# A hybrid decoder trunk on one core: the norm vector moved from the weights to x, keys joined in pairs, and a list schedule with other priorities

## The chip, the core and the metric

The kernel runs on one core of one Trainium2 chip, as one launch. The metric is the device time of a launch in microseconds (us), the median over several runs.

## The reference

The computation is a trunk of two residual layers over 1,024 positions of width 1,024, in float32. The first (even) layer splits one input projection into sliding-window attention and a state-space mixer (S5); the second (odd) layer is stick-breaking attention. Each is followed by a SwiGLU feed-forward network (FFN) of width 2,816.

```python
hn = rmsnorm(x, even_norm[i])          # x * rsqrt(mean(x^2) + eps) * gain
proj = hn @ even_w_in[i]
q, k, v, u = jnp.split(
    proj, [SWA_WIDTH, SWA_WIDTH + KV_WIDTH, SWA_WIDTH + 2 * KV_WIDTH], axis=-1)
q = rmsnorm(q.reshape(b, l, SWA_Q_HEADS, HEAD_DIM), q_norm[i])
k = rmsnorm(k.reshape(b, l, SWA_KV_HEADS, HEAD_DIM), k_norm[i])
o_attn = swa_sink_attention(q, k, v, sinks[i])
o_ssm = s5_mixer(u, ...)
mixed = jnp.concatenate([o_attn, o_ssm], axis=-1) @ even_w_out[i]
...
x = x + mixed
hn = rmsnorm(x, ffn_norm[layer])
x = x + (jax.nn.silu(hn @ ffn_w_gate[layer]) * (hn @ ffn_w_up[layer])) @ ffn_w_down[layer]
```

## The kernel before, in words

Every large product is made of three TensorE products of rounded operands: each operand is split into a high part (`hi`) and the rest (`lo`), and `mm3` (L301 to L305) adds high x high, high x low and low x high. The high part is a copy on ScalarE (ACT) or VectorE (DVE), the low part a subtraction on DVE or, for some weights, on GpSimd (POOL). TensorE (PE) also does the transposes, by a product with the identity.

**Who sets the order.** The kernel is written as tasks with an engine, an assumed duration, dependencies, tokens for buffers, and a priority `pos`. `Flow.run` (L133) is a list scheduler: it plays the tasks through once, and each time an engine is free by its assumed durations it takes the ready task with the lowest `pos` whose tokens are there. What it takes is emitted at once, so that the order of every engine, and of the DMA issues on SyncE (SP), is fixed when the kernel is built. The assumed durations only set the order; on the chip each engine goes through its list and waits where a dependency isn't met. The priorities hang on a table of constants (L59 to L77: `WKVPOS`, `S5POS`, `SWAPOS`, `LEAD`, `EVAC`, `POS1` and others).

**The even layer**, in which the edits lie (`even`, L735):

1. *Norm and transposes* (`norm`, L769). Each of the 8 tiles of x (128 rows, 512 KB) is loaded (`xt`, two buffers, L774), squared and summed on ACT (L779), and its reciprocal root `r` is made by `rstd_tasks` (L361): one small step on DVE (L367), Ln and Exp on ACT, three or four small steps on DVE (L378 to L383), and a copy into `rx` (L782). The tile itself is transposed unscaled (`psT`, L788) and split into `hh` and `hl` (L269 or L267, L795). The factor r is applied later, to the results.
2. *Weights* (`weight_tasks`, L308). The norm vector (gain) is folded into the weights of this layer. For keys and values ACT and DVE do it in four pieces each (L328, L344); for u and q POOL scales the loaded block in four pieces (`scaled`, L338), ACT takes the high part (L331) and POOL the low part (L348).
3. *Keys and values* (`kv`, L856), one tile at a time, each in a PSUM bank: 24 products (`ps_kv`), evacuation on ACT (L872, L873), a sum (L877), the root by `rstd_tasks`, the scaling of the keys on DVE (L880), one transpose (`ps_kT`, L886), a copy.
4. *u* (`u_round`, L929, twice), *q* (`q_round`, L1012, twice), each with two blocks of weights.
5. *S5* (`s5_common`, L389, then eight `s5_eighth`, L596). `s5_common` is one chain on DVE, from the transposed angles (`ps_a`, L436; the first DVE row is L441) to the tables (L541); the first product that needs it is the transpose `ps_v` (L622).
6. *Sliding-window attention* (`swa`, L1155, eight tiles: scores `ps_s`, exponentials on ACT, `ps_pT`, `ps_o`), and the *GLU* of S5 (`ps_g`, L1285; sigmoid on ACT). Exp and Sigmoid lie in different ACT table sets; `Trunk.act` (L243) puts a table load (L249) wherever the set changes in ACT's order.
7. *Output projection* in two halves (`ps_wo`), then the norm of half 0 with its transposes (`psT`, L1515, `hn`), then that of half 1 with the sums for the FFN (`T`, L1596 to L1613).

The FFNs (`ps_gu`, L1679, and `ps_d`, L2013) and the odd layer (`odd_tasks`, L2086) follow in the same schedule. The two FFNs are dense stretches of 128x512 products.

Of the kernel before, what the change touches and what calls it, by code (L numbers as in the profile page):

```python
# [107 lines left out]
class Flow:  # L108
# [110 lines left out]
class Trunk:  # L219
# [88 lines left out]
    def weight_tasks(self, fl, src, a, b, pos, deps=(), engines=("POOL", "POOL"), wtok=("w8",),  # L308
                     rtok=("raw",), gain=None, pool=None, tile_=None):
# [13 lines left out]
        def hi():  # L323
            st["w"] = tile_() if tile_ else (pool or self.wp).tile([P, 2, a, b], F32R, tag="w8", name="w8")
            if folded:
                for k in range(4):
                    part = slice(m * k, m * k + m)
                    nc.scalar.activation(out=st["w"][:, 0, part], in_=st["raw"][:, part], func=AF.Copy,  # L328
                                         scale=gain[:, k:k + 1])
            elif engines[0] == "ACT":  # L330
# [4 lines left out]
        def scaled():
            for k in range(4):
                part = st["raw"][:, m * k:m * k + m]
                nc.gpsimd.tensor_scalar(out=part, in0=part, scalar1=gain[:, k:k + 1], scalar2=None, op0=ALU.mult)  # L338

        def lo():  # L340
            if folded:
                for k in range(4):
# [1 line left out]
                    nc.vector.scalar_tensor_tensor(out=st["w"][:, 1, part], in0=st["raw"][:, part],  # L344
                                                   scalar=gain[:, k:k + 1], in1=st["w"][:, 0, part].bitcast(F32),
                                                   op0=ALU.mult, op1=ALU.subtract)
                return
# [387 lines left out]
    def even(self, right):  # L735
# [22 lines left out]
        fl.tokens(xt=XT, uc=1, uT=2, t1=1, el=1, cl=2, kp=1, tp=2, rot=1, sv=1, gv=1, gw=1,  # L758
                  hv=1, yg=1, pT=2, sq=1, qn=1, kv=2)
# [8 lines left out]

        def norm(t, pos):  # L769
# [6 lines left out]
            def square():  # L776
                sq = npool.tile([P, DM], F32, tag="xn", name="xn", bufs=1)
                st["ss"] = self.smp.tile([P, 1], F32, tag="ss", name="ss")
                A.activation(out=sq, in_=st["xt"], func=AF.Square, accum_out=st["ss"])  # L779

            def keep():
                V.tensor_copy(out=rx[:, t:t + 1], in_=st["r"])  # L782

            def turn(kh):
                st[kh] = bank("B", [P, 4, P], "psT")
                for j in range(4):
# [1 line left out]
                    nc.tensor.transpose(st[kh][:, j], st["xt"][:, k * P:(k + 1) * P], self.ident)  # L788
# [1799 lines left out]
```

## Time and profile before

| what | value |
|---|---|
| median of 3 runs | 2378.26 us (2377.5 to 2378.88) |
| profiled execution, its own time | 2380.52 us |
| its span, first to last instruction | 2378.7 us |
| PE busy in the span | 2295.7 us |
| DVE, ACT, POOL busy | 1594.0, 1036.4, 598.4 us |
| granted TensorE clock, mean | 0.985 |

The profile is of one execution. A row of the timeline gives start, duration, engine, line, operation, and in brackets the idle time of the engine before it with what released it. A row of the stages gives for each engine the busy time in that stretch and the number of instructions; PEclk is the share of full clock that TensorE was granted. 1.8 us of the profiled time lie outside the span. PE is the busiest engine, and its idle time, 83.0 us in all, is what another order can save.

### The profile page before, as it was taken

To read this page: it belongs to the slowest core of one execution; us is meant where nothing else is said; L and a number is where in the kernel's file an instruction comes from. 1 tells how busy PE (TensorE), PEld (TensorE's weight loads), DVE (VectorE), ACT (ScalarE), POOL (GpSimd) and SP (SyncE) were. 2 spreads that over 40 slices of the span, in tenths; PEclk is the share of its full clock that TensorE was granted. 3 is DMA by queue.
4 is the path that set the end of the run, shared out by engine and by line. 5 is a ranking of instruction groups with operands and counts; after the bars stand their busy time and mean duration, and the time that the engine had idled before them with its cause. 6 is when DMAs were issued, how large, how long until landed. Compare 5 with 4: busy or idle time off the path is not lost.

```text
span 2378.7 us, 32679 instructions
## 1 busy us (share of the span) xinstructions
PE 2295.7 (97%) x12284; PEld 1854.1 (78%) x12284; DVE 1594.0 (67%) x2514; ACT 1036.4 (44%) x2070; POOL 598.4 (25%) x526
## 2 busy tenths in 40 slices
PE   7897999999999999999999999999989999999998
PEld 6796488888888887777877777788768888888777
DVE  7998655755555558884676766778655655556785
ACT  6276843422222233354565655665423222233332
POOL 4310000553434324400000000000243534333530
PEclk9998999999999999999999999999989999999999
DMA  5110225332323284334211111235422323248333
GB/s 148 32 36 23 75 89 196 106 106 91 114 93 115 93 309 169 98 103 128 76 37 44 45 46 45 90 122 182 144 72 93 111 89 111 89 153 294 133 107 115
DMA packets 237183, 256.89 MB, mean 108 GB/s; under 512 B 27744, under 2 KB 178272, under 8 KB 237024
## 3 DMA queue, kind: packets, MB, share of 16 engines
q1 hardware_dynamic: 237024, 254.79, 32.6%
q8 instruction: 97, 1.59, 0.3%
q14 instruction: 62, 0.51, 0.1%
HBM read 188.02 MB, written 65.54 MB: 107 GB/s over the span
## 4 chain that ended last, share of the span: by engine, by line
PE 48%; DVE 4%; issue 1%; ACT 0%; DMA 0%; POOL 0%; DVEq 0%; POOLq 0%; SPq 0%; ACTq 0%
PE ps_gu L1679 18%; PE ps_d L2013 8%; PE ps_z L2263 3%; PE ps_j L303 3%; PE ps_O L2357 3%; PE ps_j L304 2%; PE ps_j L305 2%; PE ps_v L303 1%; PE ps_T L2339 1%; PE ps_v L304 1%; PE ps_v L305 1%; PE ps_T L2338 1%; PE ps_wo L303 1%; PE ps_wo L304 1%; PE ps_wo L305 1%
## 5 line engine op out<-in xcount | busy, mean ns | idle before, releaser
L2013 PE MATMUL ps_d<-wds,hs 128*128 128x512 f32 x1848 | 436.5, 396 | 6.2 <-DVE hs L1990 6.0
L2013 PEld LDWEIGHTS ps_d<-wds,hs 128*128 128x128 f32 x1848 | 347.7, 189 | 90.5 <-DVE hs L1990 9.4
L1679 PE MATMUL ps_gu<-hnT,ws 128*128 128x512 f32 x1584 | 392.6, 393 | 0.0
L1679 PEld LDWEIGHTS ps_gu<-hnT,ws 128*128 128x128 f32 x1584 | 298.1, 188 | 69.2
L1679 PE MATMUL ps_gu<-mixO,ws 128*128 128x512 f32 x960 | 239.4, 399 | 0.2 <-DVE mixO L1619 0.2
L1679 PEld LDWEIGHTS ps_gu<-mixO,ws 128*128 128x128 f32 x960 | 182.0, 190 | 44.5 <-DVE mixO L1619 0.7
L1979 ACT ACTIVATE wds<-wds 128x1024 fp32r<-128x1024 f32 x84 | 82.9, 987 | 239.6 <-PE ps_d L2013 132.4
L1763 ACT ACTIVATE ws<-S 128x512 fp32r<-128x512 f32 x176 | 104.2, 620 | 183.1 <-PE ps_gu L1679 183.1
L1766 DVE TENSOR_TENSOR ws<-S,ws 128x512 fp32r<-128x512 f32 x176 | 172.8, 995 | 1.0 <-ACT ws L1763 0.8
L1982 DVE TENSOR_TENSOR wds<-wds,wds 128x1024 fp32r<-128x1024 f32 x84 | 118.3, 1408 | 79.0 <-ACT wds L1979 79.0
L1733 POOL TENSOR_TENSOR S<-raw 128x512 f32<-128x512 f32 x44 | 57.8, 1314 | 413.1 <-DMA raw<-in_ffn_w_up 278.4
L1990 DVE TENSOR_TENSOR hs<-rawh,hs 128x512 fp32r<-128x512 f32 x154 | 160.1, 1070 | 0.1
L2289 DVE TENSOR_TENSOR_SCAN sp<-sp,start 128x512 f32<-128x512 f32 (+5 forms) x128 | 111.0, 909 | 62.0 <-ACT sp L255 62.0
L1956 POOL TENSOR_TENSOR wds<-wds,wds 128x1024 f32<-128x1024 f32 (+1 forms) x48 | 125.2, 2629 | 94.8 <-DVE wds L1982 62.3
L1763 ACT ACTIVATE ws<-raw 128x512 fp32r<-128x512 f32 x116 | 70.7, 623 | 177.6 <-PE ps_gu L1679 174.7
L2273 POOL MEMSET sp<- 128x1 f32 x128 | 10.1, 99 | 514.7 <-PE ps_T L2338 352.3
L255 ACT ACTIVATE sp<-ps_z 128x383 f32<-128x383 f32 (+7 forms) x176 | 82.8, 520 | 88.3 <-PE ps_z L2263 87.6
L348 DVE TENSOR_TENSOR w<-raw,w 128x1024 fp32r<-128x1024 f32 x70 | 85.5, 1228 | 44.5 <-ACT w L331 43.8
L1679 PE MATMUL ps_gu<-hn,ws 128*128 128x512 f32 x432 | 112.7, 396 | 0.0
L303 PE MATMUL ps_j<-hn,w 128*128 128x512 f32 x256 | 111.1, 434 | 0.1
L1766 DVE TENSOR_TENSOR ws<-raw,ws 128x512 fp32r<-128x512 f32 x116 | 107.1, 935 | 0.2
L304 PE MATMUL ps_j<-hn,w 128*128 128x512 f32 x256 | 101.7, 397 | 1.1 <-DVE hn L1521 1.1
(430 smaller groups left out, 5037.5 us busy)
## 6 DMA issues: line engine op xcount, KB each, us to landing
rawh<-hc SPq DMA_DIRECT2D x154, 256.0 KB, 3.0
raw<-in_ffn_w_gate SPq DMA_DIRECT2D x48, 512.0 KB, 3.9
raw<-in_ffn_w_up SPq DMA_DIRECT2D x48, 512.0 KB, 3.9
hc<-hS SPq DMA_DIRECT2D x44, 512.0 KB, 3.2
wds<-in_ffn_w_down SPq DMA_DIRECT2D x40, 512.0 KB, 6.9
raw<-in_odd_w_in SPq DMA_DIRECT2D x36, 512.0 KB, 3.7
x_scratch<-x SPq DMA_DIRECT2D x22, 512.0 KB, 4.0
hc<-gu SPq DMA_DIRECT2D x22, 512.0 KB, 2.6
```

The costliest lines, as they stand in the source:

```text
L303: nc.tensor.matmul(out, ah, bh, start=start, stop=False)
L304: nc.tensor.matmul(out, ah, bl, start=False, stop=False)
L305: nc.tensor.matmul(out, al, bh, start=False, stop=stop)
L348: eng[engines[1]].tensor_tensor(out=st["w"][:, 1], in0=st["raw"], in1=st["w"][:, 0].bitcast(F32), op=ALU.subtract)
L1679: nc.tensor.matmul(st[bank], w[:, kk], h[:, s, kk], start=start and not kk and not n, stop=kk == 3 and n == 2 and not (start and bank != " ...
L1763: A.activation(out=G["w"][:, b, 0], in_=raw[n](), func=AF.Copy)
L1766: TT(out=G["w"][:, b, 1], in0=raw[n](), in1=G["w"][:, b, 0].bitcast(F32), op=ALU.subtract)
L1956: Q.tensor_tensor(out=wdv(out, q), in0=wdv(a, q), in1=wdv(b, q), op=op_)
L1982: TT(out=st["w"][:, 0:len(r), 1], in0=wdv(home[b], q), in1=st["w"][:, 0:len(r), 0].bitcast(F32), op=ALU.subtract)
L1990: TT(out=st["h", i][:, 1], in0=st["raw"][:, i], in1=st["h", i][:, 0].bitcast(F32), op=ALU.subtract)
L2013: nc.tensor.matmul(banks[tag, k], h[:, x_, ks], w[:, y_], start=start and not p and not n_, stop=p == NP - 1 and n_ == 2 and j not in (0, ...
L2289: V.tensor_tensor_scan(out=v_[:, ::-1], data0=v_[:, ::-1], data1=d1, initial=0.0 if diag else sp[:, o + n:o + n + 1], op0=ALU.mult, op1=AL ...
```

## The change

It has five parts.

1. The norm vector is no longer folded into the weights. It is loaded as a full row, broadcast to 128 partitions (512 KB in place of 4 KB), and each tile of x is multiplied by it before its transposes, in two halves of 512 columns: on DVE for tiles 0 and 1, on POOL for tiles 2 to 7. The folded branches and POOL's `scaled` are gone; the weights of keys and values are split by one ACT copy and one DVE subtraction of 128x1024 each.
2. The roots of the x tiles are made four tiles at a time (`ssx`, one set of steps for four columns). The square is written into `hl`, which is free at that time, so the low part of a tile also waits for its square.
3. Keys and values are done in pairs of tiles: one bank, one sum, one set of root steps, one more small product (`times`) and one 128x256 scaling for both. Only one pair may be in that chain at a time (`kv=1`).
4. In the scheduler, a DVE task whose function is in `SHARED` counts 1.45 times as long while POOL is busy.
5. All priorities are other numbers.

```diff
-LSTEP = (8820.91, 1139.85)
-EVAC, LEAD, ZLEAD, CLAG, SPREAD, START, LATE, BOOST = -391.73, 1726.6, 1211.15, -491.95, 0.95, 101.18, -7955.94, 0.0
+LSTEP = (7237.53, 1915.24)
+EVAC, LEAD, ZLEAD, CLAG, SPREAD, START, LATE, BOOST = -787.344, 0.419, 1312.135, -99.126, 1.119, -98.314, -14774.696, 0.0
...
+SHARED = ("vbuild", "cbuild", "rot", "scan", "back", "lo", "scale", "bstack", "phases", "powers", "lam", "bbar")
...
+                    if e == "DVE" and busy["POOL"] and getattr(fn, "__name__", "") in SHARED:
+                        us *= 1.45
...
-        def scaled():
-            for k in range(4):
-                part = st["raw"][:, m * k:m * k + m]
-                nc.gpsimd.tensor_scalar(out=part, in0=part, scalar1=gain[:, k:k + 1], scalar2=None, op0=ALU.mult)
...
-        fl.tokens(xt=XT, uc=1, uT=2, t1=1, el=1, cl=2, kp=1, tp=2, rot=1, sv=1, gv=1, gw=1,
-                  hv=1, yg=1, pT=2, sq=1, qn=1, kv=2)
+        fl.tokens(xt=XT, xg=2, uc=1, uT=2, t1=1, el=1, cl=2, kp=1, tp=2, rot=1, sv=1, gv=1, gw=1,
+                  hv=1, yg=1, pT=2, sq=1, qn=1, kv=1)
...
-        gain = cpool.tile([P, KD], F32, name="gain0")
-        t_g = add("DMA", .5, lambda: nc.sync.dma_start(out=gain, in_=io["even_norm"][0].rearrange("(k p) -> p k", p=P)),
-                  pos=-1100.0)
+        gain = npool.tile([P, DM], F32, name="gain0")
+        t_g = add("DMA", 1.7, lambda: self.bcast(gain, io["even_norm"][0]), pos=-1100.0)
...
+                A.activation(out=hl[:, :, t * P:(t + 1) * P], in_=st["xt"].rearrange("p (k n) -> p k n", k=KD),
+                             func=AF.Square, accum_out=ssx[:, t:t + 1])
+
+            def scale(kh):
+                if not kh:
+                    st["xg"] = npool.tile([P, DM], F32, tag="xg", name="xg", bufs=2)
+                cs = slice(512 * kh, 512 * kh + 512)
+                (nc.vector if t < 2 else nc.gpsimd).tensor_tensor(out=st["xg"][:, cs], in0=st["xt"][:, cs], in1=gain[:, cs], op=ALU.mult)
...
-            fl.after([i, *ts], ["xt"])
-            i = self.rstd_tasks(fl, st, 1, 1.0 / DM, i, pos + RXLAG[0])
-            rx_done.append(add("DVE", .07, keep, [i], pos=pos + RXLAG[0]))
+            fl.after([i, *gs], ["xt"])
+            fl.after(ts, ["xg"])
+            sqd = i
+            squares.append(i)
+            if t % 4 == 3:
+                g, sg = slice(t - 3, t + 1), {"ss": ssx[:, t - 3:t + 1]}
+                i = self.rstd_tasks(fl, sg, 4, 1.0 / DM, squares[-4:], pos + RXLAG[0])
...
-                out.append(add("DVE", dve_us(512), lambda kh=kh: lo(kh), [i], pos=pos, give=["B"]))
+                out.append(add("DVE", dve_us(512), lambda kh=kh: lo(kh), [i, sqd], pos=pos, give=["B"]))
...
+            def times():
+                r = st["r"].rearrange("p (t b) -> p t b", t=2)
+                TT(out=r, in0=r, in1=rx[:, t0:t0 + 2].unsqueeze(2).to_broadcast([P, 2, 2]), op=ALU.mult)
...
-        kvs = [kv(t, -900.0 + 20 * t) for t in range(NT)]
+        kvs = [kv(t, -900.0 + 40 * t) for t in range(NT // 2)]
```

**What it moves.** The long runs of products of the two FFNs keep their order word for word (2,332 and 2,425 instructions of PE in one piece). The order changes in the even layer, in the odd layer and at the seams. Two engines show it best.

POOL at the beginning of the kernel, before: `raw` are blocks of weights, `w_` their split form, `gain_130` the norm vector.

```order
L846 TENSOR_SCALAR gq<-gq 128x1
L847 MEMSET mask 128x256
L848 AFFINE_SELECT mask<-mask 128x128
L850 AFFINE_SELECT mask<-mask 128x128
L338 TENSOR_SCALAR raw<-raw,gain_130 128x256 x12
L348 TENSOR_TENSOR w_690<-raw,w_690 128x1024
L348 TENSOR_TENSOR w_717<-raw,w_717 128x1024
L338 TENSOR_SCALAR raw<-raw,gain_130 128x256 x4
```

The same place now: `xt` is a tile of x, `xg` the tile times the norm vector.

```order
L766 TENSOR_TENSOR xg<-xt,gain_131 128x512
L839 TENSOR_SCALAR gq<-gq 128x1
L840 MEMSET mask 128x256
L841 AFFINE_SELECT mask<-mask 128x128
L843 AFFINE_SELECT mask<-mask 128x128
L766 TENSOR_TENSOR xg<-xt,gain_131 128x512 x11
L333 TENSOR_TENSOR w_600<-raw,w_600 128x1024
L333 TENSOR_TENSOR w_643<-raw,w_643 128x1024
```

The twelve products with x stand ahead of the first low part of the weights of u; the scalings between the low parts are gone.

DVE in front of the S5 chain, before: `kn` are the keys of a tile, `ss`, `v`, `t`, `y` the small vectors of their roots; the chain begins with `ar`.

```order
L383 TENSOR_TENSOR y<-y,t 128x2
L271 TENSOR_SCALAR kT<-ps_kT,gk 128x128
L880 SCALAR_TENSOR_TENSOR kn<-ps_kv,rx,y 128x128
L877 TENSOR_REDUCE ss_736<-kn 128x2
L367 TENSOR_SCALAR v<-ss_736 128x2
L380 TENSOR_TENSOR t<-v,y 128x2
L381 TENSOR_TENSOR t<-t,y 128x2
L382 TENSOR_SCALAR t<-t 128x2
L383 TENSOR_TENSOR y<-y,t 128x2
L877 TENSOR_REDUCE ss_770<-kn 128x2
L880 SCALAR_TENSOR_TENSOR kn<-ps_kv,rx,y 128x128
L441 COPY ar<-ps_a 128x32
```

And now: `hl` is the low part of x, `rx` the roots of four tiles, `c_439` and `d_591` constants of S5.

```order
L879 TENSOR_TENSOR kn<-ps_kv,y 128x256
L779 TENSOR_TENSOR hl<-psT,hh 128x4x128
L794 COPY rx<-y 128x4
L532 TENSOR_SCALAR c_439<-c_439 128x4x64
L533 COPY c_439<-c_439 128x4x64
L534 COPY c_439<-c_439 128x4x64
L548 TENSOR_TENSOR d_591<-ident,dT 16x512
L422 COPY ar<-ps_a 128x32
```

The key chains of the third and fourth pair now stand behind the beginning of the S5 chain, whose first row follows on the last low part of x. In all, 16 sets of root steps for x and keys become 6.

ACT in the stage where attention and GLU overlap, before: `s__2971` are the scores of one attention tile (Exp), `sg` the gates of the GLU (Sigmoid).

```order
L255 ACTIVATE s__2971,sm<-s__2971,nm 128x256 x4
L249 ACT_TABLE_LOAD
L255 ACTIVATE sg<-ps_g,bg 128x512
L249 ACT_TABLE_LOAD
L255 ACTIVATE s__2971,sm<-s__2971,nm 128x256 x4
L255 ACTIVATE m<-m 128x8
L249 ACT_TABLE_LOAD
L255 ACTIVATE sg<-ps_g,bg 128x512
```

And now:

```order
L253 ACT_TABLE_LOAD
L259 ACTIVATE s__2834,sm<-s__2834,nm 128x256 x4
L253 ACT_TABLE_LOAD
L259 ACTIVATE sg<-ps_g,bg 128x512
L253 ACT_TABLE_LOAD
L259 ACTIVATE s__2834,sm<-s__2834,nm 128x256 x4
L259 ACTIVATE m<-m 128x8
L253 ACT_TABLE_LOAD
L259 ACTIVATE sg<-ps_g,bg 128x512
L271 ACTIVATE pT<-ps_pT 128x512
```

The alternation of Exp and Sigmoid begins an attention tile earlier and goes on through more tiles: over the whole kernel there are 27 table loads where there were 22.

On PE, the transposes `psT` of the norm of half 0 stood in groups of 8 and 24 with one block of 18 output products between them; they now stand in groups of 8, 4, 4, 4 and 12 with blocks of 6, 6, 18 and 6 output products between them.

More of the change, by code (lines that the diff above doesn't have):

```diff
@@ L324, in hi @@
             st["w"] = tile_() if tile_ else (pool or self.wp).tile([P, 2, a, b], F32R, tag="w8", name="w8")
-            if folded:
-                for k in range(4):
[L327 to L330, printed above, removed]
+            if engines[0] == "ACT":
                 nc.scalar.activation(out=st["w"][:, 0], in_=st["raw"], func=AF.Copy)
@@ L854, in even, with kv, mm @@
         t_set = add("POOL", 1.5, setup2, [i], pos=-960.0)
-        def kv(t, pos):
+        def kv(i, pos):
             st = {}
-            def mm(k):
-                if not k:
-                    st["ps"] = bank("A", [P, 256], "ps_kv")
-                ts_ = slice(t * P, (t + 1) * P)
+            t0 = 2 * i
+            def mm(j, k):
+                if not k and not j:
+                    st["ps"] = bank("A", [P, 2, 256], "ps_kv")
+                ts_ = slice((t0 + j) * P, (t0 + j + 1) * P)
@@ L884, in turn @@
             def turn():
-                st["pt"] = bank("B", [P, P], "ps_kT")
-                nc.tensor.transpose(st["pt"], st["kn"].rearrange("p b d -> p (b d)"), self.ident)
+                st["pt"] = bank("B", [P, 2, P], "ps_kT")
+                for j in range(2):
+                    nc.tensor.transpose(st["pt"][:, j], st["kn"][:, j].rearrange("p b d -> p (b d)"), self.ident)
             def put():
-                self.copy(kT[:, t * P:(t + 1) * P], st["pt"], gk)
-            i = None
@@ L892, in kv @@
-            for k in range(0, KD, 2):
-                i = add("PE", 6 * mm_us(256) + (.1 if t else 0.0), lambda k=k: mm(k), [i, *normed[2 * t:2 * t + 2], wkv[k // 4][1]],
-                        pos=pos, take=[] if k else ["A"])
-            last = i
-            i = add("ACT", .5, evac, [i, rx_done[t]], pos=pos, take=["kv"])
-            i = add("DVE", .2, total, [i], pos=pos)
-            i = self.rstd_tasks(fl, st, 2, 1.0 / HD, i, pos)
-            i = add("DVE", dve_us(128), mul, [i], pos=pos, give=["A"])
@@ L900, in kv @@
-            i = add("PE", .12, turn, [i], pos=pos, take=["B"], give=["kv"])
-            i = add(EITHER, any_us(128), put, [i, t_set], pos=pos, give=["B"])
-            return last, i
-        kvs = [kv(t, -900.0 + 20 * t) for t in range(NT)]
+                self.copy(kT[:, t0 * P:(t0 + 2) * P].rearrange("p (t c) -> p t c", t=2), st["pt"], gk)
+            last = None
+            for j in range(2):
+                for k in range(0, KD, 2):
+                    last = add("PE", 6 * mm_us(256) + (.1 if i else 0.0), lambda j=j, k=k: mm(j, k),
+                               [last, *normed[2 * (t0 + j):2 * (t0 + j) + 2], wkv[k // 4][1]], pos=pos + 20 * j,
+                               take=[] if k or j else ["A"])
@@ new lines, in kv @@
+            n = add("ACT", 1.0, evac, [last, rx_done[t0]], pos=pos, take=["kv"])
+            n = add("DVE", .4, total, [n], pos=pos)
+            n = self.rstd_tasks(fl, st, 4, 1.0 / HD, n, pos)
+            n = add("DVE", .15, times, [n], pos=pos)
+            n = add("DVE", dve_us(256), mul, [n], pos=pos, give=["A"])
+            n = add("PE", .23, turn, [n], pos=pos, take=["B"], give=["kv"])
+            n = add(EITHER, any_us(256), put, [n, t_set], pos=pos, give=["B"])
+            return last, n
@@ L905, in even @@
+        kvs = [kv(t, -900.0 + 40 * t) for t in range(NT // 2)]
         fl.after([a for a, _ in kvs], ["w8"])
-        kv_done = [b for _, b in kvs]
+        kv_done = [b for _, b in kvs for _ in range(2)]
         def to_ep():
@@ L912, in to_ep @@
             box["tp"] = [box["ep"].tile([P, 4, P], F32, name=f"tp{i}") for i in range(2)]
-        t_ep = add(None, 0.0, to_ep, normed + common["all"] + [a for a, _ in kvs])
+        t_ep = add(None, 0.0, to_ep, normed + common["all"] + kv_done)
         class Lazy:
@@ L930, in u_round @@
             st = {}
-            w = [self.weight_tasks(fl, w_in[:, 4 * i:4 * i + 4, 768 + 256 * r:1024 + 256 * r], 4, 256, pos - WQLEAD[0], [t_g],
-                                   engines=("ACT", "POOL"), gain=gain[:, 4 * i:4 * i + 4]) for i in range(2)]
+            w = [self.weight_tasks(fl, w_in[:, 4 * i:4 * i + 4, 768 + 256 * r:1024 + 256 * r], 4, 256, pos - WQLEAD[0], [],
+                                   engines=("ACT", "POOL")) for i in range(2)]
             def mm(j, h, k):
@@ L1019, in halves @@
                                     for b in range(2)]
-            w = [self.weight_tasks(fl, halves(i), 8, 128, pos - WQLEAD[1], [t_g], engines=("ACT", "POOL"), gain=gain[:, 4 * i:4 * i + 4])
+            w = [self.weight_tasks(fl, halves(i), 8, 128, pos - WQLEAD[1], [], engines=("ACT", "POOL"))
                  for i in range(2)]
```

87 lines of the change are left out of this document (37 added, 50 removed).

## The prediction

> **What bounds the kernel now.** I read the page's totals first, then a table by stage, then the timeline of PE where it is idle.
>
> ```profile
> span 2378.7 us, 32679 instructions
> PE 2295.7 (97%) x12284; PEld 1854.1 (78%) x12284; DVE 1594.0 (67%) x2514; ACT 1036.4 (44%) x2070; POOL 598.4 (25%) x526
> ```
>
> PE works for 97% of the span. The change takes no product away from it, so only its 83.0 us of idle time (2378.7 - 2295.7) can go, and the time that it loses at a lower clock. The table by stage says where these are; its columns are the length, the busy time of PE, PEld, DVE, ACT and POOL, the granted clock and the DMA.
>
> ```profile
> 0.00:46.00 46.00, 35.00 (x257) 34.00 (x257) 30.15 (x111) 31.00 (x83) 12.56 (x32) 0.93 0.66 168
> 46.00:62.00 16.00, 9.74 (x43) 7.97 (x44) 14.89 (x38) 5.48 (x16) 14.39 (x12) 0.89 0.30 85
> 93.00:203.00 110.00, 107.28 (x820) 99.32 (x818) 98.45 (x205) 63.91 (x145) 15.00 (x10) 0.98 0.10 26
> 203.00:308.00 105.00, 88.94 (x469) 50.59 (x469) 79.66 (x230) 80.89 (x202) 0.00 (x0) 0.92 0.19 63
> 308.00:460.00 152.00, 146.42 (x1065) 133.07 (x1064) 90.98 (x163) 68.20 (x140) 28.71 (x18) 0.97 0.41 133
> 1110.00:1540.00 430.00, 430.00 (x2883) 334.93 (x2884) 286.26 (x409) 249.45 (x569) 8.54 (x105) 1.00 0.18 55
> 1680.00:1745.00 65.00, 50.99 (x246) 40.28 (x243) 48.02 (x72) 33.47 (x60) 31.76 (x22) 0.90 0.39 127
> ```
>
> PE is idle for 11.0 us up to 46, for 6.3 up to 62, for 2.7 between 93 and 203, for 16.1 in the stage of attention and GLU, for 5.6 around the norm of half 0, for nothing in most of the odd layer, and for 14.0 at the seam to the second FFN. The edits lie in the first 203 us. There these waits of PE count:
>
> ```profile
> 13.44 1.94 PE L788 MATMUL psT<-ident,xt 128*128 128x128 f32 x8 [4.55 <-DMA xt<-in_x]
> 49.98 0.44 PE L886 MATMUL ps_kT<-ident,kn 128*128 128x128 f32 x1 [4.28 <-DVE kn L880]
> 55.91 0.33 PE L886 MATMUL ps_kT<-ident,kn 128*128 128x128 f32 x1 [1.20 <-DVE kn L880]
> 61.51 0.30 PE L886 MATMUL ps_kT<-ident,kn 128*128 128x128 f32 x1 [1.07 <-DVE kk L485]
> 92.58 1.09 PE L622 MATMUL ps_v<-ident,t 128*128 128x128 f32 x4 [5.22 <-issue]
> 171.53 0.39 PE L304 MATMUL ps_q<-w,hh 128*128 128x256 f32 x1 [1.09 <-POOL w L348]
> ```
>
> All but the first and last are waits for DVE: for the keys, and at 92.58 for the end of the S5 chain. So the question is how much earlier DVE can begin that chain (it begins at 51.63, below) and get through it.
>
> **The opening: what goes, comes and moves.** On DVE these groups of the first 62 us are cut (count, busy, mean ns):
>
> ```profile
> L383 DVE TENSOR_TENSOR y<-y,t 128x1 f32<-128x1 f32 (+1 forms) x16 | 5.4, 340 | 0.6
> L367 DVE TENSOR_SCALAR v<-ss 128x1 f32<-128x1 f32 (+1 forms) x16 | 4.5, 293 | 0.6 <-ACT xn L779 0.4
> L380 DVE TENSOR_TENSOR t<-v,y 128x2 f32<-128x2 f32 x8 | 3.8, 478 | 0.9 <-ACT y L255 0.8
> L344 DVE SCALAR_TENSOR_TENSOR w<-raw,gain,w 128x256 fp32r<-128x256 f32 x8 | 3.3, 477 | 0.0
> L382 DVE TENSOR_SCALAR t<-t 128x1 f32<-128x1 f32 (+1 forms) x16 | 3.2, 197 | 0.5
> L880 DVE SCALAR_TENSOR_TENSOR kn<-ps_kv,rx,y 128x128 f32<-128x128 f32 x8 | 2.7, 340 | 0.1
> L877 DVE TENSOR_REDUCE ss<-kn 128x2 f32<-128x128 f32 x8 | 2.2, 277 | 3.4 <-ACT kn L873 3.4
> L381 DVE TENSOR_TENSOR t<-t,y 128x2 f32<-128x2 f32 x8 | 1.7, 214 | 0.3
> L378 DVE SCALAR_TENSOR_TENSOR t<-v,y 128x1 f32<-128x1 f32 x8 | 1.7, 211 | 1.1 <-ACT y L255 1.1
> L782 DVE COPY rx<-y 128x1 f32<-128x1 f32 x8 | 1.1, 143 | 0.0
> L795 DVE TENSOR_TENSOR hl<-psT,hh 128x512 fp32r<-128x512 f32 x16 | 10.6, 686 | 1.8 <-ACT hh L267 1.8
> ```
>
> The first ten sum to 29.6 us. What comes in their place: 6 sets of root steps of about 0.9 us (five or six small rows of 0.15 to 0.2), 5.4; 2 copies and 4 small products, 0.9; 4 sums and 4 key scalings of 128x256 at an estimated 0.4 and 0.5 (between the 128x128 rows above and the 686 ns of a 128x512 one), 3.6; two subtractions of weights at the 1228 ns of L348, 2.5; four products of x at the 686 ns of L795, 2.8. That is 15.2, and DVE saves 14.4 us.
>
> Half of the old 29.6 was not work, as the next rows show: the same kind of step took 0.16 us at 22.78 and 2.26 at 47.12.
>
> ```profile
> 22.78 0.16 DVE L383 TENSOR_TENSOR y<-y,t 128x1 f32<-128x1 f32 x1
> 47.04 4.65 POOL L348 TENSOR_TENSOR w<-raw,w 128x1024 fp32r<-128x1024 f32 x2
> 47.12 2.26 DVE L383 TENSOR_TENSOR y<-y,t 128x2 f32<-128x2 f32 x1
> 49.51 0.33 DVE L880 SCALAR_TENSOR_TENSOR kn<-ps_kv,rx,y 128x128 f32<-128x128 f32 x1
> 51.63 0.18 DVE L441 COPY ar<-ps_a 128x32 f32<-128x32 f32 x1
> 59.59 3.70 POOL L338 TENSOR_SCALAR raw<-raw,gain 128x256 f32<-128x256 f32 x4
> 59.66 0.42 DVE L381 TENSOR_TENSOR t<-t,y 128x2 f32<-128x2 f32 x1
> L338 POOL TENSOR_SCALAR raw<-raw,gain 128x256 f32<-128x256 f32 x32 | 33.3, 1057 | 27.8 <-DMA raw<-in_even_w_in 27.7 <-POOL raw L338 0.2
> 411.63 1.29 POOL L1603 TENSOR_TENSOR T<-T,R 128x512 f32<-128x512 f32 x1
> ```
>
> A step on two SBUF operands waits out the POOL subtraction (2.26 of its 2.33 us), one that reads PSUM (L880) doesn't, and beside POOL's scaling (L338) a step takes 0.42, some 0.25 more than alone. The 33.3 us of scaling on POOL go; they blocked DVE little, but the low parts of the weights of u stood behind them. POOL's new products with x are two-operand instructions of 128x512, 1.29 us each by the last row, twelve of them in the some 23 us in which x comes in: POOL is busy for two thirds of that time. By the new order 24 small DVE steps stand between the first product of x and the S5 chain, the last eleven of them behind most of POOL's products. I charge 13 steps with two thirds of half a product, 0.44 us each, 6 us with rounding. The ends are 0 (all fall into gaps) and 24 x 1.29 = 31 (each meets a whole product).
>
> The Trainium skill (SBUF — State Buffer, Who interferes with whom) says that a DVE instruction with two SBUF inputs is fully blocked by a GpSimd instruction that reads SBUF, and that issue order decides who blocks. The trace agrees at 47.12 (2.26 us); at 59.66 it took 0.42 beside POOL pieces of 0.92, less than a full block. By that rule, with every step behind a running product, the opening would cost the 31 and not the 6, which is the rival below.
>
> So the S5 chain begins 14.4 - 6 = 8.4 us earlier on DVE. Two key chains of some 2 us that stood ahead of it now stand within it, as two did before, only longer; I take 7. PE has to follow: the three waits for keys (4.28 + 1.20 + 1.07 = 6.6) go, since the weights of u no longer stand behind the scalings. The start is even: 1 MB more of weights and gain is issued ahead of the first x (some 2.8 us at 360 GB/s, an estimate from the 512 KB loads), and the first keys no longer stand behind the third tile's transposes (4.55 us of waiting). **Opening: -7 us**, from 0 (DVE blocked by 13 rather than 6) to -14 (no blocking).
>
> **To 203.** The wait of 1.09 us for a low part on POOL goes: **-1**.
>
> **Attention and GLU, 203 to 308.** Nothing here gets cheaper, and the order has five table loads more:
>
> ```profile
> L249 ACT ACT_TABLE_LOAD x21 | 26.9, 1283 | 0.4
> ```
>
> 5 x 1.283 = 6.4 us on ACT, which is busy for 80.9 of 105 us. I take them as mostly hidden, and the reordered rest as no help: **-1**, from +6.4 to -10 (16.1 of idle time and the clock of 0.92 mostly recovered).
>
> **The norm of half 0.** PE waits for DVE here (idle 5.6 in the stage) and the clock is 0.97 of 152 us, 4.6 us lost. 36 products that stood elsewhere now stand between the transposes, as cover: **-5**, from 0 to -8.
>
> **The odd layer and the seams.** The two FFNs keep their order, so nothing is due there. The odd layer has no idle time to lose between 1110 and 1540; its order is new, and so is that of the seam, where 14.0 us are idle. Both signs are possible: **0**, from +8 to -8.
>
> The sum is -7 - 1 - 1 - 5 = **-14**. From the profiled execution's 2380.5 (span 2378.7 and 1.8 around it) that gives 2366.5; the median of the runs is 2.2 us lower, so 2364.
>
> **The rivals.** *POOL's products block DVE* (slower). Place: the 24 small steps between 8 and 45 us. Price: up to 31 us in place of 6, so that the S5 chain begins 31 - 14.4 = 17 us later than now, and `ps_v` with it; the other terms give 7 back: 2388. It decides from 0.6 us a step on top of what I charged (14 over 24). For it: 2.26 at 47.12. Against it: POOL waits for x a third of the time, and eleven steps stand late. *The table loads are not hidden*: +6.4 in place of -1, 2372. For it: each stands between two things that PE waits for. *The chain is bound elsewhere*: `ps_a` is an instruction of PE at the end of the key products, and the parameters of S5 are loaded behind x; if these hold the chain at its old time, the opening gains nothing, and with half of the norm's term the sum is -3: 2375, no change that can be measured. *The new order fits much better*: opening -12, attention and GLU -10, norm -7: 2349. For it: DVE's locks were what the old order did not know of.
>
> **How the numbers follow.** Chances: forecast 0.46, much better 0.20, table loads 0.12, no change 0.12, slower 0.10. A measurement of this kernel tells about 0.2%, 4.8 us, from no change. Faster by more: 0.46 + 0.20 and most of the table loads' 0.12, 0.76; within: 0.13; slower: 0.11. The range leaves a tenth on each side: its low end lies near the fourth rival, since the odd layer's term may add to the forecast, its high end reaches past the case of no change: 2346 to 2381.
>
> **What would show it.** Right: L422, the chain's first row, at 43 to 46 us; the `ps_v` transpose near 85; no wait for `kn` over 1 us; the small steps under POOL's products at 0.6 us in the mean; PE idle in the norm of half 0 under 2 us. Wrong: small DVE steps of 1.3 us in a row before 40; a longer stretch from the first scores to the first output product with ACT busy in nearly all of it; idle time in the odd layer.

## The result and the profile after

| what | before | after |
|---|---|---|
| median of 4 runs each | 2378.24 us | 2355.74 us (2354.62 to 2356.55) |
| ratio, 95% interval | | 0.9905 (0.9888 to 0.9922) |
| profiled execution, its span | 2378.7 us | 2354.8 us |
| PE busy, idle in the span | 2295.7, 83.0 us | 2285.4, 69.4 us |

The kernel became 22.5 us faster, 14 of which were forecast. The number of products is the same; PE lost 13.6 us of its idle time, and its busy time fell by 10.3 us: less work ran at a low clock (the mean granted clock of the profiled execution is 0.992, it was 0.985). First the page's totals of the kernel after:

```profile
span 2354.8 us, 32617 instructions
PE 2285.4 (97%) x12284; PEld 1844.0 (78%) x12284; DVE 1598.9 (68%) x2441; ACT 1045.4 (44%) x2064; POOL 584.8 (25%) x506
```

The table by stage of the kernel after, with the borders that were used before (length; busy time of PE, PEld, DVE, ACT, POOL; granted clock; DMA):

```profile
0.00:46.00 46.00, 32.34 (x245) 31.02 (x246) 29.78 (x64) 27.37 (x57) 20.68 (x35) 0.96 0.67 179
46.00:62.00 16.00, 14.87 (x80) 12.33 (x79) 15.24 (x56) 6.33 (x13) 4.65 (x2) 1.00 0.41 99
93.00:203.00 110.00, 105.80 (x829) 97.95 (x828) 102.08 (x228) 66.28 (x155) 7.47 (x3) 0.98 0.10 25
203.00:308.00 105.00, 91.27 (x472) 49.40 (x471) 74.53 (x215) 88.73 (x216) 0.00 (x0) 0.97 0.18 63
308.00:460.00 152.00, 147.71 (x1056) 136.42 (x1055) 91.79 (x151) 63.56 (x122) 34.67 (x22) 0.98 0.43 139
1110.00:1540.00 430.00, 430.00 (x2867) 330.99 (x2863) 291.39 (x414) 258.71 (x596) 8.74 (x108) 1.00 0.18 55
1680.00:1745.00 65.00, 57.70 (x269) 46.22 (x268) 54.11 (x79) 31.48 (x59) 36.21 (x26) 0.95 0.32 102
```

The same clock times hold other work in the two kernels, so that the rows compare only roughly (the seam of the second FFN ends at 1720 now). Marks in the work are better. From the timelines of the two kernels (us from the start of the span):

| mark | before | after | difference |
|---|---|---|---|
| first row of the S5 chain on DVE (`ar`) | 51.63 | 44.59 | -7.0 |
| first transpose `ps_v` on PE | 92.58 | 84.10 | -8.5 |
| first scores `ps_s` | 202.97 | 191.95 | -11.0 |
| first product of the first FFN (`ps_gu` from `hn`) | 425.54 | 415.22 | -10.3 |
| end of the first FFN (last `ps_d`) | 1091.16 | 1078.17 | -13.0 |
| end of the last transpose before the dense part of the second FFN | 1743.94 | 1719.67 | -24.3 |
| end of the span | 2378.7 | 2354.8 | -23.9 |

The timeline of DVE in the opening of the kernel after:

```profile
14.10 1.22 DVE L333 TENSOR_TENSOR w<-raw,w 128x1024 fp32r<-128x1024 f32 x1
20.59 1.13 DVE L364 TENSOR_TENSOR y<-y,t 128x4 f32<-128x4 f32 x1
21.76 1.22 DVE L794 COPY rx<-y 128x4 f32<-128x4 f32 x1
25.85 1.21 DVE L348 TENSOR_SCALAR v<-ss 128x4 f32<-128x4 f32 x1
27.57 0.16 DVE L361 TENSOR_TENSOR t<-v,y 128x4 f32<-128x4 f32 x1
27.96 1.16 DVE L363 TENSOR_SCALAR t<-t 128x4 f32<-128x4 f32 x1
29.16 1.19 DVE L364 TENSOR_TENSOR y<-y,t 128x4 f32<-128x4 f32 x1
44.59 0.19 DVE L422 COPY ar<-ps_a 128x32 f32<-128x32 f32 x1 [1.99 <-PE ps_a L417]
```

POOL's products with x in the same stretch:

```profile
20.39 2.56 POOL L766 TENSOR_TENSOR xg<-xt,gain 128x512 f32<-128x512 f32 x2 [0.66 <-DMA xt<-in_x]
24.49 2.54 POOL L766 TENSOR_TENSOR xg<-xt,gain 128x512 f32<-128x512 f32 x2 [1.54 <-DMA xt<-in_x]
27.76 2.57 POOL L766 TENSOR_TENSOR xg<-xt,gain 128x512 f32<-128x512 f32 x2 [0.73 <-DMA xt<-in_x]
```

Five small steps on DVE wait for one product of POOL each (1.13 to 1.22 in place of 0.16) and end when it ends; the one at 27.57 falls between two pairs of products and takes 0.16. At 44.59 DVE has been idle for 1.99 us: the chain waits for PE, for `ps_a` near the end of the key products, and no longer for DVE. PE in the same stretch and at the next marks:

```profile
8.75 2.79 PE L772 MATMUL psT<-ident,xg 128*128 128x128 f32 x12 [8.75 <-DVE xg L766]
32.75 0.66 PE L885 MATMUL ps_kT<-ident,kn 128*128 128x128 f32 x2 [3.07 <-DVE kn L879]
52.39 0.41 PE L885 MATMUL ps_kT<-ident,kn 128*128 128x128 f32 x2 [1.13 <-DVE ui L465]
76.33 0.44 PE L885 MATMUL ps_kT<-ident,kn 128*128 128x128 f32 x2 [1.82 <-DVE c L522]
84.10 0.60 PE L603 MATMUL ps_v<-ident,t 128*128 128x128 f32 x4
372.10 1.25 PE L1516 MATMUL psT<-ident,xn 128*128 128x128 f32 x8 [1.62 <-DVE hn L1522]
374.43 0.58 PE L307 MATMUL ps_wo<-wox,mixA 128*128 128x256 f32 x1 [1.08 <-DVE hn L1522]
```

The waits for keys are still there, 6.0 us in three pieces; they stand elsewhere. What is gone is the second wait for x (4.55) and the 5.22 at `ps_v`; against that the first transposes start 3.4 us later (8.75, before 5.32), since weights and the whole row of the norm vector are loaded ahead of x, and x is multiplied first. The seam before the second FFN, on PE, in the kernel before and then in the kernel after:

```profile
1729.49 2.88 PE L1613 MATMUL psT<-ident,T 128*128 128x128 f32 x12 [4.97 <-DVE T L1596]
1735.81 4.04 PE L1613 MATMUL psT<-ident,T 128*128 128x128 f32 x20 [2.55 <-DVE T L1596]
```

```profile
1629.33 1.73 PE L2358 MATMUL ps_O<-wt,v 128*64 128x256 f32 x16
1703.81 1.70 PE L1614 MATMUL psT<-ident,T 128*128 128x128 f32 x12 [1.29 <-DVE T L1597]
1706.64 0.66 PE L1614 MATMUL psT<-ident,T 128*128 128x128 f32 x4 [1.13 <-POOL T L1601]
1708.42 4.10 PE L1614 MATMUL psT<-ident,T 128*128 128x128 f32 x20 [1.12 <-DVE T L1597]
```

The last two waits of 4.97 and 2.55 have become waits of 1.1 to 1.3. The odd layer's attention ends some 50 us earlier (last `ps_O` at 1679.73 before, 1629.33 now), 13 of them from before the odd layer, and 180 output products stand behind it in PE's order where 48 stood: they are cover for the sums that the transposes wait for. From the end of the first FFN to the end of this seam PE is idle for 13.1 us where it was 21.5; 4.0 of these 8.4 us come from the waits just shown, the rest from other waits on the way.

### The profile page after: what moved, and what is told of

It reads as the page before. It is cut to its first block, busy times and chain, and to the rows that moved or that the text cites. A ratio compares the mean times of both kernels' runs of the same rounds, so it can differ in the third digit from the quotient of the medians.

```text
span 2354.8 us, 32617 instructions
## 1 busy us (share of the span) xinstructions
PE 2285.4 (97%) x12284; PEld 1844.0 (78%) x12284; DVE 1598.9 (68%) x2441; ACT 1045.4 (44%) x2064; POOL 584.8 (25%) x506
## 4 chain that ended last, share of the span: by engine, by line
PE 84%; DVE 9%; ACT 4%; issue 2%; DMA 0%; SPq 0%; DVEq 0%; ACTq 0%
PE ps_gu L1680 36%; PE ps_d L2014 15%; PE ps_z L2264 3%; PE ps_O L2358 3%; PE ps_j L307 3%; PE ps_wo L307 3%; PE ps_j L309 2%; PE ps_j L308 2%; PE ps_wo L308 2%; PE ps_wo L309 2%; PE ps_v L307 2%; DVE hs L1991 1%; PE ps_T L2340 1%; PE ps_T L2339 1%; PE ps_v L308 1%
## 5 line engine op out<-in xcount | busy, mean ns | idle before, releaser
L1767 DVE TENSOR_TENSOR ws<-S,ws 128x512 fp32r<-128x512 f32 x176 | 187.4, 1088 | 3.8 <-ACT ws L1764 3.5
L1983 DVE TENSOR_TENSOR wds<-wds,wds 128x1024 fp32r<-128x1024 f32 x84 | 124.3, 1479 | 79.8 <-ACT wds L1980 79.4
L1991 DVE TENSOR_TENSOR hs<-rawh,hs 128x512 fp32r<-128x512 f32 x154 | 152.4, 1018 | 2.2 <-ACT hs L1988 2.1
L1767 DVE TENSOR_TENSOR ws<-raw,ws 128x512 fp32r<-128x512 f32 x116 | 115.3, 994 | 1.1 <-ACT ws L1764 0.9
L307 PE MATMUL ps_j<-hn,w 128*128 128x512 f32 x256 | 111.5, 436 | 0.0
L328 ACT ACTIVATE w<-raw 128x1024 fp32r<-128x1024 f32 x80 | 83.8, 1059 | 52.3 <-PE ps_wo L309 32.6
L259 ACT ACTIVATE gu<-gu 128x512 f32<-128x512 f32 x66 | 41.7, 632 | 139.7 <-DVE gu L1809 65.5
```

Of the source, the lines that this page charges most:

```text
L307: nc.tensor.matmul(out, ah, bh, start=start, stop=False)
L1767: TT(out=G["w"][:, b, 1], in0=raw[n](), in1=G["w"][:, b, 0].bitcast(F32), op=ALU.subtract)
L1983: TT(out=st["w"][:, 0:len(r), 1], in0=wdv(home[b], q), in1=st["w"][:, 0:len(r), 0].bitcast(F32), op=ALU.subtract)
L1991: TT(out=st["h", i][:, 1], in0=st["raw"][:, i], in1=st["h", i][:, 0].bitcast(F32), op=ALU.subtract)
```

## The experiments

The theory of the prediction is that the joined steps shorten DVE's work ahead of the S5 chain and that the chain then starts earlier; the new numbers are worth little by themselves. Its first rival is that the numbers make the gain and the edits only go with them; after the first four runs a third reading came up, that PE's key products and the weights that they wait for set the chain's start. Twelve kernels were timed, four to eleven executions each. All in one table (the median of before was 2378.1 to 2378.7 beside them):

| run | what it is | median us | ratio to before, 95% interval |
|---|---|---|---|
| 1 | after, odd layer's numbers of before | 2370.4 | 0.9967 (0.9955 to 0.9980) |
| 2 | after, even layer's numbers of before | 2369.7 | 0.9964 (0.9952 to 0.9977) |
| 3 | before, odd layer's numbers of after | 2367.9 | 0.9956 (0.9943 to 0.9970) |
| 4 | after, all numbers of before | 2382.0 | 1.0013 (1.0004 to 1.0022) |
| 5 | run 2 with WKVPOS of after | 2353.9 | 0.9894 (0.9881 to 0.9907) |
| 6 | after without the factor 1.45 | 2371.0 | 0.9971 (0.9960 to 0.9981) |
| 7 | after, all products with x on DVE | 2364.7 | 0.9944 (0.9932 to 0.9956) |
| 8 | after, keys tile by tile | 2370.6 | 0.9962 (0.9951 to 0.9974) |
| 9 | run 3 with WKVPOS of after | 2365.2 | 0.9940 (0.9928 to 0.9953) |
| 10 | run 5 without the factor 1.45 | 2366.6 | 0.9951 (0.9938 to 0.9963) |
| 11 | run 5, keys tile by tile | 2361.6 | 0.9929 (0.9916 to 0.9941) |
| 12 | after with WKVPOS of before | 2366.3 | 0.9952 (0.9938 to 0.9965) |

### Numbers or edits: runs 1 to 4

Run 1 and run 3 exchange the numbers of the odd layer and the seams, from after to before and the other way round:

```diff
-WLEAD = 75.806
-LSTEP = (7237.53, 1915.24)
-POOL1, WL, HL, SL = 1.5, 78.117, 60.792, 40.702
-EVAC, LEAD, ZLEAD, CLAG, SPREAD, START, LATE, BOOST = -787.344, 0.419, 1312.135, -99.126, 1.119, -98.314, -14774.696, 0.0
+WLEAD = 30.0
+LSTEP = (8820.91, 1139.85)
+POOL1, WL, HL, SL = 1.5, 150.0, 40.0, 30.0
+EVAC, LEAD, ZLEAD, CLAG, SPREAD, START, LATE, BOOST = -391.73, 1726.6, 1211.15, -491.95, 0.95, 101.18, -7955.94, 0.0
...
-POS1 = 41333.441
-POS0 = 52615.655
+POS1 = 18000.0
+POS0 = 22000.0
```

> The kernel after, with the numbers that set the odd layer and the seams (LSTEP, EVAC, LEAD, ZLEAD, CLAG, SPREAD, START, LATE, WL, HL, SL, WLEAD, POS0, POS1) those of before. PE's order is the same up to the end of the first FFN. Theory A, two separate parts: the even layer keeps its 10.3 us and the 13.6 us that the odd layer and its seams won are lost: 2355.7 + 13.6 = 2369, first FFN product at about 415, last transposes before the second FFN at about 1733. Theory B, the later stages gain because the even layer hands over earlier or better: nothing is lost, 2356 to 2358.

> The kernel before, with the new numbers for the odd layer and the seams alone; none of the edits. Theory A, a separate part: 2378.2 - 13.6 = 2364.6. Theory B, only with the new even layer: 2378 to 2380.

Run 1 lost 14.6 us, run 3 won 10.2 without any edit, 3.4 less than theory A's 13.6. Theory A holds in the main: the odd layer and its seams are a separate part. PE in run 1, at its last transposes:

```profile
1717.53 1.09 PE L1614 MATMUL psT<-ident,T 128*128 128x128 f32 x4 [4.96 <-DVE T L1597]
1724.68 1.94 PE L1614 MATMUL psT<-ident,T 128*128 128x128 f32 x16 [2.47 <-DVE T L1597]
```

The two waits of before are back, to a tenth of a microsecond (4.97 and 2.55), and 48 output products stand behind the last `ps_O` again. In run 3 it is 180, as in the kernel after. Which of the numbers does it is open.

Run 2 exchanges the even layer's numbers, run 4 all of them:

```diff
-WKVPOS = (-1262.48, -977.59)
-RXLAG = (133.0, 0.0)
...
+WKVPOS = (-1008.68, -929.18)
+RXLAG = (19.66, 0.0)
...
```

> The kernel after, with the even layer's numbers (WKVPOS, RXLAG, QPOS, GPOS, S5POS, SWAPOS, S5LEAD, WQLEAD, GLUPOS) those of before; from the first FFN on the order of PE is the same. Theory A, the joined steps by themselves make the even layer shorter: most of the 10.3 us stays, 2356 to 2360, the S5 chain's first row at 43 to 46. Theory B, the new numbers make it and the edits only suit them: 2355.7 + 10.3 = 2366 or more, the chain's first row at 50 or later.

> The kernel after with all numbers of before, so that only the edits and the factor of 1.45 remain. Theory A: the loss of the first and the second run added, 2370 to 2374, faster than before by 4 to 8. Theory B: without the numbers the edits bring nothing, 2378 or more.

Both went by theory B. With all the old numbers the edits, with the factor, made the kernel a little slower (0.13%), and run 2 lost 14 us. The opening of run 2 shows why, DVE first, then PE:

```profile
23.16 2.18 DVE L333 TENSOR_TENSOR w<-raw,w 128x1024 fp32r<-128x1024 f32 x1
55.84 0.19 DVE L422 COPY ar<-ps_a 128x32 f32<-128x32 f32 x1 [3.75 <-PE ps_a L417]
```

```profile
17.31 1.12 PE L772 MATMUL psT<-ident,xg 128*128 128x128 f32 x4 [2.11 <-POOL xg L766]
25.40 0.58 PE L308 MATMUL ps_kv<-w,hh 128*128 128x256 f32 x1 [1.96 <-DVE w L333]
52.23 0.66 PE L885 MATMUL ps_kT<-ident,kn 128*128 128x128 f32 x2 [3.26 <-DVE kn L879]
```

The second block of weights for keys and values is split at 23.16 in place of 14.10 (and takes 2.18, beside a product of POOL). The key products wait for it (1.96), and until it is there they can't fill PE's waits for products of x on POOL (2.11 at 17.31, 1.15 behind it). `ps_a` stands behind them on PE, and the chain waits 3.75 us for `ps_a`. In the kernel before, the chain followed on DVE's own work. So the edits moved the bound of the opening from DVE to PE's key products. The late block is not the whole of the delay, though: up to the chain's first row PE is idle for 18.7 us in run 2 and for 13.7 in the kernel after, 5.0 of the 11.3 us by which the row comes later. The rest is busy time, at a granted clock of 0.84 in place of 0.96 and with six key products more ahead of `ps_a`; the wait for keys at 52.23 (3.26) has its like in the kernel after (3.07 at 32.75).

### One pair of numbers: runs 5, 9 and 12

Run 5 is run 2 with `WKVPOS = (-1262.48, -977.59)`; run 12 is the kernel after with `WKVPOS = (-1008.68, -929.18)`; run 9 has no edits.

> The kernel of the second run (the even layer's numbers of before) with one pair of them new again: WKVPOS, the places of the two blocks of weights for keys and values. Theory C: in the second run the key products waited until 25.4 for the second block, and the S5 chain's first row waited 3.75 us for the product ps_a behind them; with the block split early the chain begins at 45 to 47 and the time is some 9 us less, 2361. Theory D, DVE's small steps and their order hold the chain: its first row stays at 53 or later, 2368 to 2370.

> The kernel after with only WKVPOS as before. Theory C: the second block of weights comes late again, the key products wait to 25, the chain's first row is at 52 to 56 and 11 to 15 us are lost: 2367 to 2371. The rival, the other new numbers of the even layer make up for it: 2356 to 2360.

> The kernel of the third run (the kernel before with the new numbers of the odd layer, no edits) with the new WKVPOS as well. Theory C: before, the key products waited for x and its low parts and never for the second block of weights, so that nothing is gained: 2366 to 2370 as in the third run. The rival, splitting that block early is what wins, with or without the edits: 2354 to 2358.

Run 5 gained 15.8 us over run 2 (9 were forecast), and with that was as fast as the kernel after or a little faster (the intervals 0.9881 to 0.9907 and 0.9888 to 0.9922 overlap). Run 12 lost 10.6. In its profile 4.8 us of the loss stand at `ps_v` (88.87), 7.1 at the first scores and 11.0 at the first FFN product, so that not all of it arises in the opening. The first rows of the chain in runs 5 and 12:

```profile
14.02 1.21 DVE L333 TENSOR_TENSOR w<-raw,w 128x1024 fp32r<-128x1024 f32 x1
42.40 0.19 DVE L422 COPY ar<-ps_a 128x32 f32<-128x32 f32 x1 [1.75 <-PE ps_a L417]
```

```profile
22.24 2.22 DVE L333 TENSOR_TENSOR w<-raw,w 128x1024 fp32r<-128x1024 f32 x1
52.61 0.19 DVE L422 COPY ar<-ps_a 128x32 f32<-128x32 f32 x1 [2.25 <-PE ps_a L417]
```

So of all the even layer's new numbers this pair carries the whole gain; the rest (eight sets) are worth nothing that these runs can tell. Without the edits and the factor the pair brings little: run 9 is 2.8 us under run 3, with overlapping intervals. The pair is what lets edits and factor pay. It sets the places of both blocks, their loads too; which of these counts most was not separated.

### Keys in pairs, and POOL's products: runs 7, 8 and 11

Run 7 puts all products with the norm vector on DVE:

```diff
-                (nc.vector if t < 2 else nc.gpsimd).tensor_tensor(out=st["xg"][:, cs], in0=st["xt"][:, cs], in1=gain[:, cs], op=ALU.mult)
+                nc.vector.tensor_tensor(out=st["xg"][:, cs], in0=st["xt"][:, cs], in1=gain[:, cs], op=ALU.mult)
```

> The kernel after, with all sixteen products of x and the norm vector on DVE, none on POOL. DVE does 12 x 0.69 = 8.2 us more before the S5 chain and meets no product of POOL. Theory C, the chain waits for PE and DVE had gaps of some 9 us: first row of the chain at 45 to 48, 2356 to 2360. The rival of the prediction, POOL's products are what holds DVE: first row at 42 or earlier, 2352 or less. DVE full: first row at 52, 2363.

It took 2364.7, 9 us more than the kernel after. The chain's first row stands at 47.68 (44.59), after 2.95 us of waiting for `ps_a`, so that the place was forecast and the cost was too low; `ps_v` comes at 92.05, 8 us later, and why the delay grows to that is open. POOL's products cost less than the same work on DVE: what they hold back isn't what bounds the opening.

Runs 8 and 11 have the old key chains (`kv` with one tile, `kv=2`) in the kernel after and in run 5:

```diff
...
-        kvs = [kv(t, -900.0 + 40 * t) for t in range(NT // 2)]
+        kvs = [kv(t, -900.0 + 20 * t) for t in range(NT)]
...
```

> The kernel after, with keys and values one tile at a time again (eight chains of roots in place of four, two at a time in the chain); numbers, roots of x in fours and the products with the norm vector stay. Theory C, the joining of small DVE steps isn't what moved the chain: its first row within 2 us of 44.6, 2354 to 2360. Theory D: some 4 sets of steps more ahead of the chain, first row at 49 or later, 2362 or more.

> The kernel of the fifth run with keys and values one tile at a time again, as in the eighth run. Theory D, joined DVE steps bring the chain forward: first row at 48 or later, 2362 to 2370. Theory C, only the early block of weights did: first row at 41 to 45, 2352 to 2357.

The chain's first row moved to 52.32 in run 8 and to 46.23 in run 11, without a wait for `ps_a` in either: DVE bounds it there, by 7.7 and 3.8 us. The times rose by 14.8 and 7.7. Run 8 went by theory D; run 11 fell between its two forecasts in the place (46.23) and next to D's in the time (2361.6). Theory C, that the early block alone does it, falls: both are needed. With the block late the joined steps gain nothing (run 2 took 2369.7, run 3 without the edits 2367.9); with the steps apart the early block gains part.

### The factor of 1.45: runs 6 and 10

```diff
-SHARED = ("vbuild", "cbuild", "rot", "scan", "back", "lo", "scale", "bstack", "phases", "powers", "lam", "bbar")
+SHARED = ()
```

> The kernel after, with no function in SHARED, so that the factor of 1.45 is gone; all numbers as they are. Theory C, the factor only moves where single tasks fall and the numbers do the work: 2355 to 2359. The rival, the schedule needs it because DVE really is slower beside POOL: half of the even layer's gain or more is lost, 2361 or more.

> The kernel of the fifth run with no function in SHARED. The sixth run took the factor out of the kernel after and lost 15 us between the start of attention's inputs and the first scores. Theory F, the factor is worth that much by itself because DVE really is slower beside POOL: 2364 to 2371 here too. Theory G, the loss there came from one unlucky order: 2352 to 2358 here.

Both lost, 15.3 and 12.7 us: not one unlucky order, since the two kernels have different numbers. The factor changes no product, only the order and, with it, which of ACT and DVE makes some copies. Most of the loss lies between `ps_v` and the first scores, where POOL splits weights beside the S5 tables: this stretch takes 117.5 us in run 6 (107.9 in the kernel after) and 124.7 in run 10 (106.2 in run 5, whose profiled execution was its fastest, 2349.5). In run 6 another 4.9 us come up to the first FFN product; in run 10 3.4 are given back. PE by stretches up to 190 in run 10 (it is busy throughout from there to its first scores at 207.19), and up to 187 in run 5 (first scores at 187.84):

```profile
82.00:110.00 28.00, 24.59 (x144) 20.65 (x145) 24.86 (x41) 8.33 (x17) 2.49 (x1) 0.94 0.19 49
110.00:150.00 40.00, 36.44 (x271) 34.08 (x270) 34.55 (x55) 20.47 (x35) 5.14 (x2) 0.96 0.05 9
150.00:190.00 40.00, 35.07 (x274) 33.04 (x273) 35.21 (x81) 26.48 (x70) 2.67 (x1) 0.91 0.16 47
```

```profile
82.00:110.00 28.00, 28.00 (x177) 23.86 (x175) 26.92 (x44) 9.53 (x19) 2.36 (x1) 1.00 0.19 50
110.00:150.00 40.00, 39.05 (x325) 37.14 (x324) 37.36 (x71) 24.53 (x49) 5.34 (x2) 1.00 0.08 22
150.00:187.00 37.00, 36.70 (x315) 35.93 (x314) 34.98 (x81) 28.80 (x83) 2.63 (x1) 1.00 0.11 34
```

In the stretches shown PE is idle for 11.9 us in run 10 and for 1.3 us in run 5. Its waits in run 10 are for single steps of the S5 tables on DVE:

```profile
90.58 1.83 PE L621 MATMUL ps_k<-cl,bst 128*16 128x128 f32 x8 [2.95 <-DVE cl L616]
124.40 0.49 PE L693 MATMUL ps_y<-cl,hv 128*128 128x128 f32 x2 [3.56 <-DVE hv L686]
169.39 1.12 PE L603 MATMUL ps_v<-ident,t 128*128 128x128 f32 x4 [3.21 <-DVE t L598]
```

Ahead of each wait DVE steps of the S5 tables were held by a subtraction of POOL. The last two of these places in run 10:

```profile
117.93 5.14 POOL L333 TENSOR_TENSOR w<-raw,w 128x1024 fp32r<-128x1024 f32 x2 [33.43 <-ACT w L328]
118.15 2.72 DVE L684 TENSOR_TENSOR sv<-gw,sn 128x512 f32<-128x512 f32 x1
120.80 2.82 DVE L685 TENSOR_TENSOR gv<-gv,ct 128x512 f32<-128x512 f32 x1
166.11 2.67 POOL L333 TENSOR_TENSOR w<-raw,w 128x1024 fp32r<-128x1024 f32 x1 [43.04 <-issue]
166.61 2.72 DVE L598 TENSOR_TENSOR t<-t,t 128x512 f32<-128x512 f32 x1
```

Such a step takes 0.69 by itself (L686 at 123.66). `cbuild` (L616), `back` (L684 to L686) and `vbuild` (L598) are functions that the change named in `SHARED`. The schedule without the factor believes them done when they are not. In run 5 POOL's subtractions hold as many DVE steps in this stretch, five from 79 to 153, and PE has other work there. Run 9, without edits and without the factor, took 2365.2, run 10, with the edits and without the factor, 2366.6: edits and factor together are worth some 11 us (run 9 to run 5), the edits without the factor nothing (run 9 to run 10). What the factor would bring to the kernel before wasn't tried, so that a gain of the factor alone isn't excluded. Nor were the norm vector on x and the roots of four tiles at a time taken back by themselves.

## Why the prediction was right, and where not

**The opening, -7.** The size was right, as far as single profiles tell: the chain's first row came 7.0 us earlier (44.59; 43 to 46 was forecast) and `ps_v` 8.5 us earlier (84.1; 85); run 1, with the same order up to there, has 41.92 and 81.42. Two of its steps were not. "PE has to follow: the three waits for keys (4.28 + 1.20 + 1.07 = 6.6) go": they did not go (6.0 us now); PE's 8.5 us are 5.9 less idle time up to `ps_v` (22.5 idle of 92.58 before, 16.6 of 84.10 now) and 2.6 less busy time, at a granted clock of 0.96 in place of 0.93 and with six products fewer ahead of it. And the sum took DVE's work alone for the bound. In fact DVE was early by 2 us at the chain, PE's key products set its start, and with the old places of the two blocks of weights the gain at the chain is gone (55.84 and 52.61 in runs 2 and 12, 51.63 before), though `ps_v` in run 12 still comes at 88.87. The wait for `ps_a` stood in the rivals only, at the right place; of its two causes the key products held and the late load of the parameters did not. Its sum was given as -3; by its own terms (0, -1, -1 and half of -5) it is -4.5, 2374.

**POOL's products, 6 us.** Five steps were held for 1.13 to 1.22 us, 5.1 us over their 0.16; 13 were charged, at half the price each. All 24 small steps from 18 to 41 us took 9.1 us, 0.38 in the mean (0.6 was forecast). The slower rival at 2388, every step behind a product, did not happen: twelve of the 24 steps (from 37.11 on) come behind POOL's last product, which ended at 35.55, and the other seven fall for the most part into gaps where POOL waits for x. By the Trainium skill (SBUF — State Buffer, Who interferes with whom) copies and tensor_scalar can be blocked too, in their two-port modes; the rows at 21.76, 25.85 and 27.96 agree, with 1.16 to 1.22 us, and the prediction had spoken of two-operand steps only, though the profile before had such a row ahead of the chain (L367 at 49.76, 1.95 us beside POOL's subtraction).

**To 203, -1.** It was -2.5 between `ps_v` and the first scores, and not by the step that was given: the wait of 1.09 for the low part is gone, but PE's idle time there is 2.7 us before and 3.1 after; the rest is busy time, at a granted clock of 1.00 in place of 0.98. What decides this stretch was not seen in advance: without the factor it is 117.5 us long (run 6, 83.8 to 201.3) where it was 110.4 before and 107.9 after. The prediction priced the factor at nothing. It named it once, as the reason for the fourth rival ("DVE's locks were what the old order did not know of"), and runs 6 and 10 bear that reason out: the factor is worth 12.7 to 15.3 us, in a stretch other than the ones that the rival added up.

**Attention, GLU and the norm of half 0, -1 and -5.** From the first scores to the first FFN product it took 222.6 us before, 223.3 after and 223.6 in run 5. So these 6 us did not come. The norm's waits on PE fell only from 4.3 to 2.7 us (rows at 372 and 374; under 2 was forecast). The cover was also counted too high: of the 36 products that now stand between the transposes, 18 stood there before. The table loads, in the kernel after and in run 5, each with one more at the kernel's start:

```profile
L253 ACT ACT_TABLE_LOAD x26 | 33.4, 1283 | 0.5
```

```profile
L253 ACT ACT_TABLE_LOAD x18 | 23.1, 1283 | 0.3
```

Eight loads less, 10.3 us of ACT, and a stage of the same length: the loads were hidden, as forecast, though the alternation bought nothing either.

**The odd layer and the seams, 0.** This term failed. It was given from +8 to -8 and was -13.6: 2.7 within the first FFN (665.6 us from its first product to its end before, 663.0 now, with the same idle time and the same products; why is open) and 11.3 from there to the end of the second seam, less 0.3 given back. Of the 11.3 us 8.4 are idle time of PE and the rest busy time. The step that failed: "its order is new, and so is that of the seam, where 14.0 us are idle. Both signs are possible", and with that 0. The order of the seam could be read in advance. 180 output products behind the last `ps_O` in place of 48 are cover for waits of 4.97 and 2.55 us, which the timeline of before showed; runs 1 and 3 confirm the numbers of the odd layer and the seams by themselves at 10 to 15 us, though the cover at these two waits explains only 4.0 us of it.

So the even layer gave 10.3 of the forecast 14, the seams 13.6 of the forecast 0, and the sum of 22.5 us fell inside the range, between the forecast and its most favourable rival. That is in part luck: more than half of the gain came from a term that was put at nothing, and the even layer's part depended on the factor, which was not priced.

## What to carry to other kernels

When an edit takes work from the engine that bounds a stage, look for what is second in line and when that gets its operands: here 11 us hung on one pair of numbers, the places of two blocks of weights. In a list schedule, durations that depend on what another engine does belong in the model: without a stretch of 1.45 for DVE beside POOL, the edits here were worth nothing (run 10 against run 9). And the order around a seam can be read like a trace: count the independent products between the last producer and the waiting transposes, before and after.

## What the hardware showed beside that

A DVE step behind a POOL product waits for that one product only: at 20.59, 21.76, 27.96 and 29.16 two steps in a row each waited out one of two products in a row. The loss is one product for each step, not one for the whole row, and it falls to nothing in the gap at 27.57. Two executions with the same order of PE up to the first FFN (the kernel after and run 1) had their first `ps_v` at 84.1 and 81.4: single profiles of the opening differ by 2.7 us (PE's idle time up to the chain 13.7 and 11.7, its granted clock 0.96 and 1.00), so that differences of 2 us in it say nothing. What POOL does matters too: in the kernel before, beside eleven scalings in a row (35.67 to 46.16), small two-operand steps on DVE took 0.15 to 0.35, where a subtraction held one for 2.26.
